# Stick-breaking attention over two key blocks with a flagged full pass, and seven products for all k, q, v and g projections

## The chip, the core and the metric

The kernel runs on one core of a Trainium2 chip. A core has a matrix engine (TensorE, PE in the profile; PEld are its weight loads), a vector engine (VectorE, DVE), a scalar engine for activation functions and copies (ScalarE, ACT), a general engine (GpSimd, POOL) and a sequencer that issues most transfers (SyncE, SP). 16 DMA engines move data between the device's memory and the on-chip buffers. Each engine works through its own instructions in order and waits on semaphores for the others. The metric is the time of one execution on the device in microseconds; lower is better.

## The reference, cut to what matters

The network has two layers over 2048 positions of width 1024. Layer 0 is a gated short convolution. Layer 1 is attention with 8 heads of width 64 which has no softmax: a query's weight on a key is the key's own sigmoid times the product of (1 - sigmoid) over all keys between that key and the query. All keys and values come from one projection, queries and a gate from another, both of layer 0's output.

```python
z = jnp.einsum("bhqd,bhkd->bhqk", qb, kf[:, :, :kl]) * scale
mask = jnp.arange(kl)[None, :] < q_pos[:, None]
log_one_minus = jnp.where(mask, jax.nn.log_sigmoid(-z), 0.0)
rev = lax.cumsum(log_one_minus, axis=3, reverse=True)
weights = jnp.exp(jnp.where(mask, z + rev, -jnp.inf))
outs.append(jnp.einsum("bhqk,bhkd->bhqd", weights, vf[:, :, :kl]))
...
factors = {'norm_kv': 7.745, 'norm_b': 8.0, 'norm_f': 2.922}
```

The factors enlarge the gains of the norms ahead of k and v, of q and g, and of the last norm. Computed from the reference's inputs, the scores z of the last head and block have a standard deviation of 60.

## The kernel before

Positions are reversed on the host, so that the causal direction runs forwards within a row, and cut into four chunks of 512 (`CH`); the width is cut into 8 blocks of 128 (`KD`). Activations lie with the width on the partitions. Each f32 operand of a product is split into a high and a low part (`split`: a copy to ACT's rounding type, then a difference on DVE), and a product of three matmuls (high-high, high-low, low-high) stands for one f32 product (`mm3`).

**Stages.** The mixer's input projection, the convolution and the mixer's output projection run first, over pairs of chunks (0, 1) and (2, 3). Where a pair is taken together, two blocks of weights and two chunks make a 2 by 2 block product, which `fast_unit` does in seven block products instead of eight, from combined operands (`fast_operands`, names op_b and op_t) and combined weights (`fast_weights`: a11, a12, a22, s1 to s4). Each of the seven is 4 k-blocks times three matmuls of 512 columns, so a unit has 84 matmuls where the plain way has 96.

**k, q, v, g.** For chunks 0 and 1, `pair_operands` builds the operands (tag `kq`) and eight units follow: `pair_kq(i)` for a block of k and one of q, `pair_vg(i)` for v and g. For chunks 2 and 3, `norm_1` normalises a chunk, and `proj_k`, `proj_q`, `proj_v` and `proj_g` do plain products (tiles pk, pq, pv, pg; 24 matmuls for each block and chunk). k, q, v and g of all chunks go to device memory (k_d, q_d, v_d, sg_d).

**Attention** (`attention`, lines 1086 to 1146) runs for each chunk c and head h, and within it over all key chunks kc from c down to 0. For each of the four 128-query blocks it computes scores against 512 keys (z), ACT makes sigmoid(-z) (R), POOL masks the diagonal block, and DVE's scan turns R into running products, starting from the carry (cy) of the key chunk before. PE transposes R block by block (wt), the result is split (wth, wtl) and multiplied with v (av). v is stored as differences of neighbouring rows, so the running products alone weigh it. The tiles q2, kt and vv have two buffers each; every other key chunk's k and v go into wraw buffers.

**Output.** `out_b(c)` gates the heads' result (og), multiplies it with the output weights (tiles pob) and adds the residual; `out_norm(c)` normalises and stores. Chunk 3 has its own `out_b_last` and `finish`, whose last part is the tail of the program.

**Order.** Nothing runs as it is recorded. Every operation goes into a `Recorder` under a part's name (`part("a00", attention, 0, 0, ot)` and the like); `PLAN` gives each part a start and an end key, and `order` picks the operation that could start first by a table of costs, and the one with the lower key among equals. The result is one fixed list for each engine. So a change of parts or keys moves instructions throughout the program. All recorded operations have the one source line 355 in the profile, and are told apart by their tiles.

Of the kernel before, what the change touches and what calls it, by code (L numbers as in the profile page):

```python
# [10 lines left out]
F32 = mybir.dt.float32  # L11
# [8 lines left out]
NH = 8  # L20
# [3 lines left out]
NR, NT, NL, NWB, NRAW, NA, NWTS = 13, 4, 5, 8, 4, 16, 2  # L24
# [7 lines left out]
XNL = (0, 3, 6)  # L32
# [29 lines left out]
}  # L62

# [26 lines left out]
class View:  # L90
# [36 lines left out]
    def extent(self):  # L127
# [6 lines left out]
        for name, args, kw in self.steps:  # L134
            if name == "__getitem__":
                both = [x[args[0]] for x in both]
            elif name == "rearrange":
                both = [x.reshape(x.shape[0], -1) for x in both]
# [225 lines left out]
def kernel(  # L364
# [46 lines left out]
    v_first = const.tile([P, NCH, NH // 2, 4], F32, name="v_first")  # L411

# [257 lines left out]
    HOMES = {"b11": ["R"] * 8, "t1": ["R"] * 5 + ["wth"] * 2 + ["wtl"], "t2": ["act"] * 4, "b22": ["act"] * 4,  # L670
# [4 lines left out]
    def operand(c, nm, k, raw, eng=nc.vector):  # L675

        if k == 0:
            fast_b[c, nm] = []
            other = {"t1": "t4", "t4": "t1"} if c == "kq" else {}
# [117 lines left out]
    def share(key, d, gain):  # L797
        if gain is not None:
            split_d[key[0]], split_d[key[1]] = [d["a11"], d["a12"]], [d["a21"], d["a22"]]

    def fast_weights(c, nm, key, srcs=None, gain=None):
# [7 lines left out]
        kept_w = ("a11", "a12", "a21", "a22") if gain is not None else NAMES  # L809
        d = {n: dram.tile([P, 2, Q, P], F32, name=f"sw_{n}_{nm}") for n in kept_w}  # L810
        share(key, d, gain)
        if gain is None:
            split_d[key] = d

        def put(n, raw):
            w[n] = w_tile(f"{n}_{nm}")
            split(w[n][:, 0], w[n][:, 1], raw)
            if n in d:
                nc.sync.dma_start(out=d[n], in_=w[n].bitcast(F32))

        a = raw_blocks(nm, srcs, gain)
        if gain is not None:
            put("a21", a["a21"])
        combine(a, put)
        return w

    def prepare(nm, key, srcs, gain=None):
# [11 lines left out]
        if gain is not None:  # L839
            put("a21", a["a21"])  # L840
# [510 lines left out]
```

## Time and profile before

| | us |
|---|---|
| median of 3 runs | 1653.89 |
| lowest and highest run | 1652.05, 1655.34 |
| span of the profiled execution, first to last instruction | 1652.7 |
| first product of k, q, v, g (pair kq) | 796.7 |
| first score of attention | 963.7 |
| last product of attention with v | 1618.4 |

No time of its own is given for the profiled execution beside its span. The profile lists, for each group of instructions, the tiles (out<-in), the shape, how many there are, how long the group was busy in all, the mean of one in ns, and behind the second bar how long the engine had been idle before them and what ended that wait. A table by stretches gives, for each stretch, each engine's busy time with its count of instructions, then the granted share of PE's clock, the mean busy share of the 16 DMA engines and the GB/s that they moved. The chain of waits is followed back from the last instruction, at each step to what released it. Matmuls overlap each other, so the mean of one is longer than the distance between two.

### The profile page before, as it was taken

To read this page: it belongs to the slowest core of one execution; us is meant where nothing else is said; L and a number is where in the kernel's file an instruction comes from. 1 tells how busy PE (TensorE), PEld (TensorE's weight loads), DVE (VectorE), ACT (ScalarE), POOL (GpSimd) and SP (SyncE) were. 2 spreads that over 40 slices of the span, in tenths; PEclk is the share of its full clock that TensorE was granted. 3 is DMA by queue.
4 is the path that set the end of the run, shared out by engine and by line. 5 is a ranking of instruction groups with operands and counts; after the bars stand their busy time and mean duration, and the time that the engine had idled before them with its cause. 6 is when DMAs were issued, how large, how long until landed. Compare 5 with 4: busy or idle time off the path is not lost. (4 is left out here: it accounts for less than half of the span.)

```text
span 1652.7 us, 24087 instructions
## 1 busy us (share of the span) xinstructions
PE 1614.5 (98%) x7828; PEld 1337.6 (81%) x7828; DVE 1334.0 (81%) x1968; ACT 786.0 (48%) x1483; POOL 487.9 (30%) x684
## 2 busy tenths in 40 slices
PE   7999999999999999999999999999999999999996
PEld 5878888888888887888788878888888888888875
DVE  6999777796765559495977577988999999989995
ACT  6454444443332224242454345655655675756552
POOL 5331000010000201235512132344533344257533
PEclk9999999999999999999999999999999999999997
DMA  9487888889799999999786799998776776699644
GB/s 281 171 268 276 297 280 274 273 272 371 259 315 386 358 372 325 366 339 339 241 283 237 263 353 337 335 312 262 239 237 215 243 236 207 188 339 320 197 144 134
DMA packets 243822, 460.41 MB, mean 279 GB/s; under 512 B 23024, under 2 KB 96752, under 8 KB 243696
## 3 DMA queue, kind: packets, MB, share of 16 engines
q1 hardware_dynamic: 214336, 400.10, 70.4%
q10 hardware_dynamic: 29200, 58.74, 12.1%
q8 instruction: 62, 1.02, 0.2%
q14 instruction: 64, 0.52, 0.1%
q0 software_dynamic: 160, 0.02, 0.1%
HBM read 287.08 MB, written 171.70 MB: 278 GB/s over the span
## 5 line engine op out<-in xcount | busy, mean ns | idle before, releaser
L355 DVE TENSOR_TENSOR_SCAN R<-R,cy,ones 128x512 f32<-128x512 f32 x192 | 247.6, 1316 | 0.9 <-ACT R L355 0.6
L355 ACT CAST wth<-wt 128x512 fp32r<-128x512 f32 (+2 forms) x320 | 154.7, 527 | 159.7 <-PE wt L355 133.2
L355 DVE TENSOR_TENSOR wtl<-wt,wth 128x512 fp32r<-128x512 f32 (+2 forms) x320 | 180.1, 597 | 27.6 <-ACT wth L355 26.0
L355 PE MATMUL z<-kt,q 128*128 128x512 f32 (+2 forms) x640 | 179.7, 378 | 1.0 <-DMA kt<-k_d 0.6
L355 ACT ACTIVATE R<-z 128x512 f32<-128x512 f32 (+2 forms) x320 | 158.7, 548 | 30.8 <-PE z L355 23.7
L355 PE MATMUL wt<-ident,R 128*128 128x128 f32 x1088 | 163.9, 272 | 1.1 <-DVE R L355 1.1
L355 PEld LDWEIGHTS wt<-ident,R 128*128 128x128 f32 x1088 | 132.5, 140 | 20.8 <-DVE R L355 1.8
L355 POOL COPY halo<-p 128x2 f32<-128x2 f32 x32 | 16.1, 503 | 433.5 <-DVE p L355 433.5
L355 POOL COPY cy<-R 128x1 f32<-128x1 f32 x192 | 93.9, 492 | 142.0 <-DVE R L355 135.3
L355 PEld LDWEIGHTS z<-kt,q 128*128 128x128 f32 x640 | 111.7, 189 | 18.7 <-ACT R L355 2.3
L355 PE MATMUL av<-wtl,vv 128*128 128x512 f32 (+1 forms) x320 | 121.6, 384 | 1.8 <-DVE wtl L355 1.8
L355 PE MATMUL av<-wth,vv 128*128 128x512 f32 (+1 forms) x320 | 119.0, 372 | 2.8 <-ACT wth L355 2.3
L355 POOL TENSOR_TENSOR acc_x<-acc_x,sq_x 128x512 f32<-128x512 f32 x52 | 75.2, 1449 | 122.4 <-ACT sq_x L355 113.9
L355 DVE TENSOR_TENSOR_SCAN R<-R,ones 128x512 f32<-128x512 f32 (+3 forms) x128 | 103.9, 844 | 3.0 <-POOL R L355 2.3
L355 PE MATMUL pob<-og,whl_ob 128*128 128x512 f32 x360 | 103.8, 401 | 0.9 <-DVE x L355 0.9
L355 POOL TENSOR_SCALAR_AFFINE_SELECT R<-R 128x128 f32<-128x128 f32 x128 | 72.7, 585 | 107.4 <-ACT R L355 104.2
L355 PE MATMUL fa_C<-op_t,whl_s_C 128*128 128x512 f32 x336 | 83.4, 389 | 0.0
L355 PE MATMUL fa_B<-op_t,whl_s_B 128*128 128x512 f32 x336 | 82.0, 389 | 0.0
L355 PEld LDWEIGHTS av<-wth,vv 128*128 128x128 f32 x320 | 60.1, 188 | 19.3 <-ACT wth L355 6.6
L355 PEld LDWEIGHTS pob<-og,whl_ob 128*128 128x128 f32 x360 | 65.2, 188 | 12.6 <-DVE x L355 1.4
L355 PEld LDWEIGHTS av<-wtl,vv 128*128 128x128 f32 x320 | 60.2, 188 | 17.2 <-DVE wtl L355 5.2
L355 PEld LDWEIGHTS fa_B<-op_t,whl_s_B 128*128 128x128 f32 x336 | 63.0, 188 | 13.2
(586 smaller groups left out, 3747.0 us busy)
## 6 DMA issues: line engine op xcount, KB each, us to landing
vv<-v_d ACTq DMA_DIRECT2D x80, 256.0 KB, 4.2
kt<-k_d ACTq DMA_DIRECT2D x80, 256.0 KB, 4.8
sw_s_C<-whl_s_C SPq DMA_DIRECT2D x32, 512.0 KB, 3.8
sw_s_B<-whl_s_B SPq DMA_DIRECT2D x32, 512.0 KB, 3.5
whl_s_o<-sw_s_o SPq DMA_DIRECT2D x32, 512.0 KB, 6.2
q<-q_d ACTq DMA_DIRECT2D x64, 256.0 KB, 5.9
sw_a_C<-whl_a_C SPq DMA_DIRECT2D x24, 512.0 KB, 3.6
sw_a_B<-whl_a_B SPq DMA_DIRECT2D x24, 512.0 KB, 3.0
```

What stands on the lines that cost most here:

```text
L355: getattr(o.engine.engine, o.name)(*map(real, o.args), **{k: real(v) for k, v in o.kw.items()})
```

## The change

Three things change, and the plan's keys with them.

**Attention over two blocks.** `attend` takes the place of `attention` in the main program. A block of 128 queries sees only its own block of keys and the next older one: 256 scores for each query, one scan of 256 columns from 1.0, no carry. For a head and chunk that is 8 score matmuls of 256 columns, 2 sigmoids and 2 masks (each over both near blocks of a tile), 4 scans, 8 transposes (7 in chunk 0), 2 splits, and 10 products with v of 256 or 128 columns. In chunks 1 to 3 the block that belongs to the chunk before is loaded in addition. POOL copies the last column of each scan into `left`, except for the query block that has no older keys.

**A flag.** `any_left` takes the maximum of `left`, adds up over the partitions whether it is above zero, and keeps it as an integer. Behind the whole main program every engine reads it; if it is not zero, attention over all keys and the output of all chunks run again.

**Seven products throughout.** Chunks 2 and 3 are done as a second pair in the same way as chunks 0 and 1; the plain projections are gone. All seven pieces of a unit's weights are stored for the second pass, where four plain pieces were stored before.

```diff
-NR, NT, NL, NWB, NRAW, NA, NWTS = 13, 4, 5, 8, 4, 16, 2
+NR, NT, NL, NWB, NRAW, NA, NWTS = 12, 4, 5, 8, 4, 16, 2
...
-    "p23": (980.0, 992.4), "g2": (972.8, 1247.5), "xn3": (991.3, 1236.4), "p30": (1188.9, 1257.1),
+    "kq22": (1033.7, 1056.5), "vg22": (1041.7, 1093.2), "kq23": (1097.9, 1102.9), "vg23": (1152.5, 1157.2),
...
+    left = const.tile([P, NCH * NH * 4], F32, name="left")
+    nc.gpsimd.memset(left, 0.0)
...
-    HOMES = {"b11": ["R"] * 8, "t1": ["R"] * 5 + ["wth"] * 2 + ["wtl"], ...
+    HOMES = {"b11": ["R"] * 8, "t1": ["R"] * 4 + ["wth"] * 2 + ["wtl"] * 2, ...
...
-        kept_w = ("a11", "a12", "a21", "a22") if gain is not None else NAMES
-        d = {n: dram.tile([P, 2, Q, P], F32, name=f"sw_{n}_{nm}") for n in kept_w}
+        split_d[key] = d = {n: dram.tile([P, 2, Q, P], F32, name=f"sw_{n}_{nm}") for n in NAMES}
...
+    def attend(c, h, ot):
...
+        if c:
+            nc.scalar.dma_start(out=kt[:, CH:CH + P].bitcast(F32), in_=k_d[c - 1][h][:, 0:P])
+            nc.scalar.dma_start(out=vt[:, 4].bitcast(F32), in_=v_d[c - 1][hb][:, hi_, 0, :, :])
+        else:
+            nc.gpsimd.memset(kt[:, CH:CH + P].bitcast(F32), 0.0)
+        rs = []
+        for i in range(2):
+            ps = psum.tile([P, CH], F32, name=f"z_{nm}_{i}", tag="z", bufs=NZ)
+            for j in range(2):
+                qi = 2 * i + j
+                for m in range(2):
+                    nc.tensor.matmul(ps[:, 2 * j * P:2 * (j + 1) * P], q2[:, m, qi * P:(qi + 1) * P], kt[:, qi * P:(qi + 2) * P],
+                                     start=m == 0, stop=m == 1, skip_group_check=True)
...
+            nc.scalar.activation(r, ps, AF.Sigmoid, scale=-0.125)
+            near = r.rearrange("p (j k) -> p j k", j=2)[:, :, 0:P]
+            nc.gpsimd.affine_select(out=near, in_=near, pattern=[[0, 2], [1, P]], base=0, channel_multiplier=-1,
+                                    compare_op=ALU.is_gt, fill=1.0)
+            for j in range(2):
+                own = r[:, 2 * j * P:2 * (j + 1) * P]
+                nc.vector.tensor_tensor_scan(out=own, data0=own, data1=ones[:, 0:1].to_broadcast([P, 2 * P]), initial=1.0,
+                                             op0=ALU.mult, op1=ALU.mult)
+            n = 1 if c == 0 and i else 2
+            at = 4 * (c * NH + h) + 2 * i
+            nc.gpsimd.tensor_copy(left[:, at:at + n], r[:, 2 * P - 1:2 * P * n:2 * P])
...
+        for i, places in enumerate((((1, 0), (1, 1), (2, 1), (2, 2)), ((3, 2), (3, 3), (0, 0), (4, 3)))):
+            if c == 0 and i:
+                places = places[:3]
...
+    def any_left():
+        most = const.tile([P, 1], F32, name="most")
+        nc.vector.reduce_max(out=most, in_=left, axis=mybir.AxisListType.X)
...
+        nc.tensor.matmul(ps[:, 0:1], ones, some, start=True, stop=True)
+        nc.vector.tensor_copy(flag, ps[:, 0:1])
...
-    part("xk", pair_operands)
+    for c in (0, 2):
+        part(f"xk{c}", pair_operands, c)
         for i in range(4):
-            part(f"p{c}{i}", proj, c, i)
-        part(f"g{c}", proj_gate, c)
+            part(f"kq{c}{i}", pair_kq, c, i)
+            part(f"vg{c}{i}", pair_vg, c, i)
...
-                part(f"a{c}{h}", attention, c, h, ot)
+                part(f"a{c}{h}", attend, c, h, ot)
...
+    some = tc.nc.values_load(flag.real()[0:1, 0:1])
+    with tc.If(some != 0, preferred_fallthrough_block=False):
...
+                    attention(c, h, ot)
...
+            out_b(c)
+            out_norm(c)
```

Three places in the order of the program. On PE, in the stage where k, q, v and g of chunks 2 and 3 are made, before: pv and pg are plain products of chunks 2 and 3 with normalised operands xn, and z, wt and av belong to attention heads.

```order
L355 MATMUL pv_2_9535<-xn_5_8907,whl_v_2_1_9249 128x512
L355 MATMUL z_1_0_0_9696<-kt_1_0_9420,q_1_1_9296 128x512 x2
L355 MATMUL z_1_0_1_9702<-kt_1_0_9420,q_1_1_9296 128x512
L355 MATMUL av_2_9706<-wth_2_0_3_9694,vv_2_0_9520 128x512
L355 MATMUL pv_2_9535<-xn_5_8907,whl_v_2_1_9249 128x512
L355 MATMUL wt_2_0_1_9715<-ident,R_2_0_0_9593 128x128
L355 MATMUL wt_2_0_1_9715<-ident,R_2_0_1_9608 128x128
L355 MATMUL z_1_0_1_9702<-kt_1_0_9420,q_1_1_9296 128x512
L355 MATMUL pg_1_9681<-xn_0_8717,whl_gg_1_0_9276 128x512
```

On PE after, at the border between the two pairs: fa_vg_0 and fd_vg_0 are units of pair (0, 1) near its end, fd_kq_2 is the first of pair (2, 3), and op_t_('kq', 2) the new operands.

```order
L353 MATMUL fa_vg_0_8746<-op_t_('kq', 0)_2_7630,whl_a_vg_0_8677 128x512
L353 MATMUL fa_vg_0_8746<-op_t_('kq', 0)_3_7663,whl_a_vg_0_8677 128x512
L353 MATMUL fa_vg_0_8746<-op_t_('kq', 0)_3_7675,whl_a_vg_0_8677 128x512
L353 MATMUL fa_vg_0_8746<-op_t_('kq', 0)_3_7663,whl_a_vg_0_8677 128x512
L353 MATMUL fd_kq_2_8901<-op_t_('kq', 2)_0_8807,whl_s_kq_2_8797 128x512 x3
L353 MATMUL fd_kq_2_8901<-op_t_('kq', 2)_1_8812,whl_s_kq_2_8797 128x512 x3
L353 MATMUL fd_kq_2_8901<-op_t_('kq', 2)_2_8833,whl_s_kq_2_8797 128x512
L353 MATMUL fd_kq_2_8901<-op_t_('kq', 2)_2_8845,whl_s_kq_2_8797 128x512
L353 MATMUL fd_kq_2_8901<-op_t_('kq', 2)_2_8833,whl_s_kq_2_8797 128x512
L353 MATMUL fd_vg_0_8722<-op_b_('kq', 0)_0_7283,whl_s_vg_0_8916 128x512 x3
```

The products of chunks 2 and 3 stand in units directly behind those of chunks 0 and 1, with no attention between them; the first scores of attention come some 400 matmul rows later, in the last unit of the second pair.

On ACT, in the attention stage, before: q, kt and vv are the loads of a head, R the sigmoids, wth the first half of a split.

```order
L355 ACTIVATE R_4_1_1_13747<-z_4_1_1_13698 128x512
L355 ACTIVATE R_4_1_2_13753<-z_4_1_2_13710 128x512
L355 ACTIVATE R_4_1_3_13757<-z_4_1_3_13735 128x512
L355 DMA vv_7_0_13764<-v_d_3_212 128x512
L355 COPY ot_3_13468<-av_7_13497 64x512
L355 CAST wth_6_0_3_13777<-wt_6_0_3_13762 128x512
L355 CAST wth_6_0_2_13783<-wt_6_0_2_13769 128x384
L355 ACTIVATE R_4_0_0_13788<-z_4_0_0_13774 128x512
L355 ACTIVATE R_4_0_1_13794<-z_4_0_1_13781 128x512
L355 ACTIVATE R_4_0_2_13802<-z_4_0_2_13786 128x512
L355 ACTIVATE sq_x_13811<-x1o_3_10277 128x512
L355 DMA q_3_1_13818<-q_d_0_205 64x1024
```

On ACT after, in the attention of chunk 0.

```order
L353 CAST wth_4_0_10436<-wt_4_0_10416 128x512
L353 ACTIVATE R_6_0_10444<-z_6_0_10428 128x512
L353 CAST wth_4_1_10455<-wt_4_1_10419 128x384
L353 ACTIVATE R_6_1_10462<-z_6_1_10439 128x512
L353 DMA q_0_7_10471<-q_d_3_198 64x1024 x2
L353 DMA kt_7_10453<-k_d_7_170 128x512
L353 COPY ot_2_10363<-av_4_10450 64x512
L353 CAST wth_0_0_10498<-wt_0_0_10486 128x512
L353 DMA vv_6_10501<-v_d_3_214 128x512
L353 CAST wth_0_1_10508<-wt_0_1_10493 128x384
```

A load now stands on ACT after every second or third copy, where before there were four to eight computing instructions between two.

On SP, at the end of the program, before and after: x_3 are the result tiles of chunk 3.

```order
L355 DMA out_dram<-x_3_1_15756 128x512
L355 DMA out_dram<-x_3_5_16223 128x512
L355 DMA out_dram<-x_3_6_16273 128x512
L355 DMA out_dram<-x_3_4_16092 128x512
L355 DMA out_dram<-x_3_7_16443 128x512
L1346 UNCONDITIONAL_BRANCH
```

```order
L353 DMA out_dram<-x_3_5_13065 128x512
L353 DMA out_dram<-x_3_6_13102 128x512
L353 DMA out_dram<-x_3_4_13059 128x512
L353 DMA out_dram<-x_3_7_13153 128x512
L1338 TENSOR_LOAD flag
L1339 COMPARE_AND_BRANCH
L1339 UNCONDITIONAL_BRANCH
```

Behind the last store, SP now reads the flag, compares and branches; the same three instructions stand at the end of every engine's list, ahead of the block that runs if the flag is set.

More of the change, by code (lines that the diff above doesn't have):

```diff
@@ L30 @@
 NLIN, NZ, NWT, NAV = 2, 3, 2, 1
-XNL = (0, 3, 6)
 YLP = (2, 5)
@@ L137, in extent @@
             elif name == "rearrange":
-                both = [x.reshape(x.shape[0], -1) for x in both]
+                if args[0] == "p (j k) -> p j k":
+                    both = [x.reshape(x.shape[0], kw["j"], -1) for x in both]
+                else:
+                    both = [x.reshape(x.shape[0], -1) for x in both]
             elif name == "unsqueeze":
@@ L678, in operand @@
             fast_b[c, nm] = []
-            other = {"t1": "t4", "t4": "t1"} if c == "kq" else {}
+            other = {"t1": "t4", "t4": "t1"} if isinstance(c, tuple) and c[0] == "kq" else {}
             home[nm] = list(HOMES[other.get(nm, nm)])
@@ L817, in put @@
             split(w[n][:, 0], w[n][:, 1], raw)
[L818 to L824, printed above, removed]
+            nc.sync.dma_start(out=d[n], in_=w[n].bitcast(F32))
+        combine(raw_blocks(nm, srcs, gain), put)
         return w
     def prepare(nm, key, srcs, gain=None):
-        split_d[key] = d = {n: dram.tile([P, 2, Q, P], F32, name=f"sw_{n}_{nm}") for n in NAMES + ("a21",)[:gain is not None]}
-        share(key, d, gain)
+        split_d[key] = d = {n: dram.tile([P, 2, Q, P], F32, name=f"sw_{n}_{nm}") for n in NAMES}
         def put(n, raw):
@@ L836, in put @@
                 nc.sync.dma_start(out=d[n][:, m], in_=hl[m].bitcast(F32))
-        a = raw_blocks(nm, srcs, gain)
-        if gain is not None:
-            put("a21", a["a21"])
-        combine(a, put)
+        combine(raw_blocks(nm, srcs, gain), put)
     def prepare_out(u):
@@ L1146, in attention @@
                 nc.vector.tensor_add(ot[osl, :], ot[osl, :], av[osl, :])
+    flag = const.tile([P, 1], I32, name="flag")
+    def any_left():
+        most = const.tile([P, 1], F32, name="most")
+        nc.vector.reduce_max(out=most, in_=left, axis=mybir.AxisListType.X)
+        some = const.tile([P, 1], F32, name="some")
+        nc.vector.tensor_scalar(out=some, in0=most.bitcast(I32), scalar1=0, scalar2=None, op0=ALU.is_gt)
+        ps = st("p_left")
+        nc.tensor.matmul(ps[:, 0:1], ones, some, start=True, stop=True)
+        nc.vector.tensor_copy(flag, ps[:, 0:1])
     og_t = {}
@@ L1313 @@
                 nc.sync.dma_start(out=og_d[c][hb], in_=ot)
+    part("fl", any_left)
     for c in range(3):
@@ L1323 @@
         nc.emit(ops)
+    some = tc.nc.values_load(flag.real()[0:1, 0:1])
+    with tc.If(some != 0, preferred_fallthrough_block=False):
+        og_t.clear()
+        acc_b.clear()
+        for c in range(NCH):
+            for hb in range(NH // 2):
+                ot = sb.tile([P, CH], F32, name=f"all_ot_{c}_{hb}", tag="ot", bufs=2)
+                for h in (2 * hb, 2 * hb + 1):
+                    attention(c, h, ot)
+                nc.sync.dma_start(out=og_d[c][hb], in_=ot)
+            out_b(c)
+            out_norm(c)
 _INS = ["xT", "norm_a", "w_in_a", "conv_a", "w_out_a", "norm_kv", "w_kv", "norm_b", "w_in_b", "w_out_b", "norm_f"]
```

123 lines of the change are left out of this document (55 added, 68 removed), and 47 rows, old and new, of the table PLAN.

## The prediction

> **What bounds the kernel now.** I read the page's first part, then the busy time by stretch, then the DMA queues.
>
> ```profile
> span 1652.7 us, 24087 instructions
> PE 1614.5 (98%) x7828; PEld 1337.6 (81%) x7828; DVE 1334.0 (81%) x1968; ACT 786.0 (48%) x1483; POOL 487.9 (30%) x684
> ```
>
> PE is busy for 98% of the span, so PE work that goes shortens the kernel until something else is full. The stretches say what is next. They are cut where the program changes: output projection of the mixer (645 to 805), k, q, v, g of chunks 0 and 1 (to 964), then attention together with k, q, v, g of chunks 2 and 3 and the last projection, and the tail from 1618.
>
> ```profile
> core 0: us, PE busy (x) PEld busy (x) DVE busy (x) ACT busy (x) POOL busy (x), PEclk, DMA share, GB/s
> 645.00:805.00 160.00, 157.61 (x702) 128.93 (x701) 113.64 (x181) 54.33 (x95) 57.14 (x41) 1.00 0.91 327
> 805.00:964.00 159.00, 158.68 (x723) 130.23 (x722) 114.68 (x183) 72.49 (x127) 38.89 (x46) 1.00 0.79 272
> 964.00:1110.00 146.00, 142.66 (x768) 119.28 (x767) 125.97 (x178) 81.21 (x175) 52.09 (x95) 1.00 1.01 332
> 1110.00:1286.00 176.00, 175.17 (x959) 147.29 (x958) 160.00 (x215) 99.16 (x210) 67.43 (x134) 1.00 0.78 242
> 1286.00:1618.00 332.00, 328.97 (x1817) 276.22 (x1815) 316.57 (x428) 206.53 (x414) 163.06 (x243) 1.00 0.72 233
> 1618.00:1652.70 34.70, 19.06 (x86) 15.46 (x84) 20.22 (x37) 8.66 (x14) 11.45 (x9) 0.76 0.36 121
> ```
>
> Two things stand there. Until 1618 PE is the bound in every stretch. And the 16 DMA engines are already full in one of them: from 964 to 1110 their share is 1.01 at 332 GB/s. Before 805 the change alters little (the same matmuls in a somewhat different order), so I leave that part as it is, to within 5 us.
>
> **The change part by part.** How far apart two matmuls start is read from the chain of waits, which runs through PE there.
>
> ```profile
> 1171.70 1.62 PE pq L355 x7
> 1177.23 0.87 PE wt L355 x8
> L355 PE MATMUL z<-kt,q 128*128 128x512 f32 x448 | 142.2, 409 | 0.9 <-DMA kt<-k_d 0.6 <-ACT R L355 0.2
> L355 PE MATMUL z<-kt,q 128*128 128x384 f32 x64 | 17.2, 341 | 0.0
> L355 PE MATMUL z<-kt,q 128*128 128x256 f32 x128 | 27.4, 291 | 0.1
> L355 PE MATMUL wt<-ident,R 128*128 128x128 f32 x1088 | 163.9, 272 | 1.1 <-DVE R L355 1.1
> L355 PE MATMUL pk<-xn,whl_k 128*128 128x512 f32 x192 | 57.7, 404 | 0.0
> ```
>
> A product of 512 columns takes 1.62/7 = 0.231 us of PE, a transpose 0.87/8 = 0.109. (The mean in a group's row, 409 ns, overlaps its neighbours.) Estimated in proportion, 384 columns are 0.174 and 256 are 0.116.
>
> Attention on PE, before: the scores are 448 x 0.231 + 64 x 0.174 + 128 x 0.116 = 129 us, the products with v have the same 640 shapes, another 129, and 1088 transposes x 0.109 are 119; together 377. After: 256 score products of 256 columns are 30 us, 248 transposes 27, 192 products with v of 256 columns 22, and 112 of 128 columns. No row has this last kind. Its nearest rows are the transpose of 128 columns, 0.109, and the 512-column product, 0.231; I take 0.109, 12 us, and keep 26 as the other end. Together 91, so **286 us of PE go**. The carries between chunks go too, with their 192 copies on POOL. One R buffer fewer costs nothing that I can see: a head takes 2 of the 12, where a chunk of a head took 4 of 13.
>
> The projections of chunks 2 and 3 are 4 groups of 192 products now and 8 units of 84 afterwards: 768 - 672 = 96, x 0.231 = **22 us of PE**. They gain operands to be built (16 differences and 28 splits, 44 on DVE, about 30 us at 0.68 each, beside PE, which has 155 us of products there) and lose 8 splits of weights (the a21 pieces). The same hand-over from one operand set to the next stands in the trace around 805 (mixer output to k and q), and PE is busy for 158.68 of 159 us there, so I charge 2 us, 20 at most, which is one unit of 84 products if the operands come a unit late.
>
> By PE alone the kernel would end at 1652.7 - 286 - 22 = 1345. That is the low end, since other engines must now do their part in less time. Sixteen units, 8 as today and 8 new, take twice the 159 us from 805, and attention begins when they end, at **1123**, because scores, carries and operands share the buffers R, wth, wtl, q2, kt and vv. What stands after 1123, engine by engine:
>
> ```profile
> L355 ACT ACTIVATE R<-z 128x512 f32<-128x512 f32 x224 | 127.6, 612 | 27.9 <-PE z L355 21.9 <-PE wt L355 4.5 <-POOL cy L355 0.4
> L355 ACT CAST wth<-wt 128x512 fp32r<-128x512 f32 x224 | 123.5, 591 | 118.1 <-PE wt L355 101.7 <-DVE R L355 6.9 <-DMA q<-q_d 3.5
> L355 ACT COPY ot<-av 64x512 f32<-64x512 f32 x32 | 18.6, 581 | 25.6 <-PE av L355 22.6 <-DMA whl_gg<-sw_a_vg 2.6
> L355 ACTq DMA_DIRECT2D q<-q_d x64: 451/463/1126, 945.8 to 1542.3; - x64
> L355 ACTq DMA_DIRECT2D kt<-k_d x80: 321/327/1559, 936.7 to 1564.4; - x80
> L355 DVE TENSOR_TENSOR_SCAN R<-R,ones 128x256 f32<-128x256 f32 x32 | 21.9, 685 | 0.2
> L355 DVE TENSOR_TENSOR wtl<-wt,wth 128x512 fp32r<-128x512 f32 x224 | 144.9, 677 | 20.9 <-ACT wth L355 19.6
> L355 DVE TENSOR_TENSOR ot<-ot,av 64x512 f32<-64x512 f32 x32 | 21.7, 678 | 7.3 <-ACT ot L355 6.9
> L355 POOL TENSOR_SCALAR_AFFINE_SELECT R<-R 128x128 f32<-128x128 f32 x128 | 72.7, 585 | 107.4 <-ACT R L355 104.2 <-PE z L355 2.6
> L355 POOL TENSOR_TENSOR acc_x<-acc_x,sq_x 128x512 f32<-128x512 f32 x52 | 75.2, 1449 | 122.4 <-ACT sq_x L355 113.9 <-DVE x L355 8.2
> L355 POOL COPY cy<-R 128x1 f32<-128x1 f32 x192 | 93.9, 492 | 142.0 <-DVE R L355 135.3 <-DVE t_x L355 2.7
> ```
>
> PE: attention 91, 384 products of the output projection x 0.231 = 89, small ones 5: 185 us. DVE: 128 scans x 0.685 = 88, 64 splits x 0.677 = 43, 32 sums x 0.678 = 22, and some 60 sums and splits of the output at 0.68 = 41: 194. ACT: 64 x 0.612 + 64 x 0.591 + 32 x 0.581 = 96, its 64 issues of q x 0.463 and 112 of k and v x 0.327 = 66, and some 75 copies, squares and scalings of the output, at 0.6 like the rows above, 45: 207. POOL: 64 masks of twice the size, between 0.585 and 1.17 each, 37 to 75; 64 small copies of what is left x 0.492 = 31; 83 two-operand operations of the output x 1.449 = 120: 188 to 226. All of them stand near 200, and none above 226.
>
> The transfers are more. A head of chunks 1 to 3 loads q (0.52 MB), k and v (0.26 each) and two blocks of 0.07: 1.18 MB; a head of chunk 0 1.05. That is 36.7 MB. The SP queue moves another 59 MB after the last weight of the units (weights of the output projection 4.2 MB a chunk, residual, x2 out and back, result 2.1 each, gates and heads). **96 MB**.
>
> ```profile
> 720.00:740.00 20.00, 20.00 (x98) 16.87 (x97) 19.63 (x50) 7.68 (x14) 3.55 (x3) 1.00 1.03 399
> q1 hardware_dynamic: 214336, 400.10, 70.4%
> q10 hardware_dynamic: 29200, 58.74, 12.1%
> ```
>
> Over the whole program, the sizes of all transfers added up, SP's queue (q1) goes from 400.1 to 404.2 MB and ACT's (q10) from 58.7 to 36.7: 4% less in a fifth less time.
>
> At what rate? 332 GB/s at a full share from 964 to 1110, where both queues run as they will; 327 at 0.91, so 359 at a full one, from 645 to 805; 399 for 20 us. I take 340, nearest to the first. 96 MB / 340 GB/s = 282 us. The Trainium skill's page "DMA: Bandwidth & Descriptors", section Specifications, gives about 358 GB/s as the limit of the memory for a core. By that figure the stage would take 268 us and the sum below would be 14 us less; the 399 of one row is above it, so here it is no cap.
>
> The sum: the stage's transfers begin a unit (20 us) ahead of 1123, at 1103. 1103 + 282 = 1385. In the tail the engines idle: today's last 34.7 us move at a share of 0.36, which loses 22 us; more results are still going out there afterwards, so I charge half, 11: 1396. At the end every engine reads the flag and branches. No row has this; between nothing and the 5.9 us that a load takes to land (its row is below) I take 2: the flag was written long before, nothing but the branch is queued behind the instruction that reads it, and only SP, last to finish, reads it on the path: **1398**. The page gives the profiled execution no time of its own beside its span; the median is 1.2 us above the span, less than the rounding here. The other added operations (one maximum, one product, a copy of 128 x 1) are off the path.
>
> The units before 1123 bear the same check: they move 106 MB (nine of it because all seven pieces of a unit's weights are now stored for the second pass) in 318 us, 333 GB/s, which is just what the full stretch carried. This is cover without reserve: every GB/s that is missing there is paid at once, 3 us for one per cent.
>
> **The rivals.** *PE stays the bound.* If DMA carries 399 as from 720 to 740, the stage is 241 us and the end 1103 + 241 + 11 + 2 = 1357, next to the 1345 of PE. For it: short peaks. Against it: the share of 1.01 at 332.
>
> *The chain of a head decides.* q, k and v have two buffers each, where now far blocks borrow four more from wraw. One head runs load, scores, ACT, mask, scan, transposes, splits, products, sum.
>
> ```profile
> q<-q_d ACTq DMA_DIRECT2D x64, 256.0 KB, 5.9
> ```
>
> 5.9 to land + 0.5 + 1.2 + 1.8 + 2.7 + 0.9 + 1.2 + 1.4 + 1.0 + 1.3 = 18 us, less about 2 where two tiles overlap; with two heads in flight 8 us a head, 32 heads 256, then the tail of 35 and the first head's 16: 1123 + 256 + 51 + 2 = 1432. A load that waits for its buffer also holds up the sigmoids and copies queued behind it on ACT, and PE waits for those. Against it: loads are issued ahead of the scores of the head before.
>
> *A cold PE.* In the last stretch PE is busy for 19.06 of 34.7 us and its granted clock is 0.76. If attention has such gaps, its 185 us stretch; at 0.76 to 245, which decides nothing, and only under 185/282 = 0.66 does PE set the end; at half the clock it is 370 and the end 1123 + 370 + 2 = 1495. The Trainium skill's "TensorE: Matmul & The Clock Gate", Part 1, says that an idle window of some 3.4 us halves the clock; the trace's last row agrees in kind.
>
> *The flag is set.*
>
> ```profile
> L355 DVE TENSOR_TENSOR_SCAN R<-R,cy,ones 128x512 f32<-128x512 f32 x192 | 247.6, 1316 | 0.9 <-ACT R L355 0.6
> ```
>
> Then all of attention and three chunks of output run again behind the branch. The price is at least what DVE now spends on three rows of attention, 248 us of scans, 145 of splits and 22 of sums, 415 in all, so 1813 or more: slower than before. It decides as soon as one of the products over a query's last 128 to 255 keys is above zero. From the reference's inputs the largest of them has the logarithm -1803, since the scores spread by 60; f32 ends at -103. So the flag should be zero, unless the chip's sigmoid does not fall as the function does, which no row shows.
>
> **How the numbers follow.** Forecast 0.50; PE bound 0.22; chain of a head 0.21; cold PE 0.04; flag set 0.03. The likeliest time is 1398. The range takes the PE sum of 1345 and the chain with a late operand set, 1432 + 20, so 1345 to 1452, and leaves out the last two cases and a little of the others. Differences under 0.2% are no change to this measurement. Faster 0.965, same 0.005, slower 0.03.
>
> **What would show it.** The DMA share over the attention stage: near 1.0 at 330 to 360 GB/s bears me out. PE busy over 95% there: the first rival. Both under 0.85, with ACT or PE waiting for q, k or v: the second. A clock under 0.7 on the page: the third. Instructions of `attention` in the trace: the flag. The units should end near 1123; if that is off by over 10 us, or the stage's 96 MB do not take about 280 us, that step was wrong.

## The result

The changed kernel takes **1444.0 us** (median of four runs, 1440.5 to 1445.0) against 1653.0 for the kernel before: the ratio is **0.873, 95% interval 0.871 to 0.875**. The prediction was 1398, from 1345 to 1452. The sign and the stage that bounds were right, and the mechanism was right in the main; the time lies inside the range, but 46 us above the forecast; most of what follows looks for these 46 us. The profiled execution has a span of 1443.1 us, so that positions in its trace can be set against the terms of the prediction directly.

The first lines of the page and its two busiest DMA queues, after:

```profile
span 1443.1 us, 19169 instructions
PE 1342.1 (93%) x6174; PEld 1105.6 (77%) x6174; DVE 978.1 (68%) x1557; ACT 579.2 (40%) x999; POOL 379.2 (26%) x447
q1 hardware_dynamic: 216352, 404.30, 80.9%
q10 hardware_dynamic: 22288, 36.72, 9.5%
```

PE lost 272 us of busy time and is busy for 93% of the span, no longer 98%. The queues moved 404.3 and 36.7 MB, where 404.2 and 36.7 had been counted beforehand. The same kind of table by stretch as before, cut where the stages of the changed kernel change:

```profile
core 0: us, PE busy (x) PEld busy (x) DVE busy (x) ACT busy (x) POOL busy (x), PEclk, DMA share, GB/s
645.00:805.00 160.00, 158.56 (x709) 130.22 (x707) 101.57 (x170) 53.70 (x92) 53.07 (x40) 1.00 0.94 337
805.00:964.00 159.00, 154.40 (x697) 126.25 (x698) 122.15 (x191) 74.62 (x132) 53.22 (x48) 1.00 0.97 340
964.00:1123.00 159.00, 157.57 (x717) 128.89 (x716) 66.76 (x102) 50.12 (x87) 14.91 (x33) 1.00 0.95 329
1123.00:1402.00 279.00, 219.48 (x1188) 182.84 (x1187) 186.96 (x309) 130.81 (x228) 135.93 (x193) 0.87 0.98 294
1402.00:1443.10 41.10, 18.68 (x82) 15.54 (x80) 18.04 (x37) 7.93 (x13) 21.38 (x17) 0.70 0.63 211
```

Up to 1123 PE is the bound as forecast (157.57 of 159 us) and the transfers just keep up. From 1123 to 1402, attention and the output projection, the DMA engines take over: share 0.98, while PE, DVE, ACT and POOL are busy for 219, 187, 131 and 136 of 279 us. That is the forecast picture but for one number: the engines carry 294 GB/s here (300 at a full share), not 340. PE's clock fell to 0.87, so that its 219 us would be 191 at full clock (204 with the last row), against 185 forecast for all that stands behind 1123.

What PE waited for in that stage, by the view of the waits:

```profile
engine line waited for: us in total, times, longest us
PE z L353 <- DMA kt<-k_d: 16.5, 9, 2.7
PE av L353 <- ACT wth L353: 9.3, 7, 4.3
PE wt L353 <- DVE R L353: 9.0, 10, 2.8
```

The largest entry is a load of k, as it must be if transfers set the pace; but the waits for steps within a head (ACT's split, DVE's scan) are together longer. So two theories were open, and the first experiments set them against each other. **A**: the stage's bytes bound it, at 294 GB/s. **B**: the chain of a head, with two buffers each for q, k and v, bounds it.

### The profile page after: what moved, and what is told of

It reads as the page before. It is cut to its first block, busy times and chain, and to the rows that moved or that the text cites. A ratio compares the mean times of both kernels' runs of the same rounds, so it can differ in the third digit from the quotient of the medians.

```text
span 1443.1 us, 19169 instructions
## 1 busy us (share of the span) xinstructions
PE 1342.1 (93%) x6174; PEld 1105.6 (77%) x6174; DVE 978.1 (68%) x1557; ACT 579.2 (40%) x999; POOL 379.2 (26%) x447
## 4 chain that ended last, share of the span: by engine, by line
PE 72%; DMA 11%; DVE 7%; issue 3%; ACT 2%; POOL 2%; SPq 0%; ACTq 0%; POOLq 0%; DVEq 0%
PE fa_B L353 11%; PE fa_C L353 10%; PE fa_kq L353 6%; PE fa_o L353 6%; PE fd_B L353 5%; PE fd_C L353 5%; PE fa_vg L353 5%; PE fd_kq L353 3%; PE fd_o L353 3%; PE fd_vg L353 3%; PE fe_C L353 3%; PE fe_B L353 3%; DMA kt<-k_d 2%; PE pob L353 2%; DMA q<-q_d 2%
## 5 line engine op out<-in xcount | busy, mean ns | idle before, releaser
L353 DVE TENSOR_TENSOR_SCAN R<-R,ones 128x256 f32<-128x256 f32 x128 | 89.5, 739 | 23.1 <-POOL R L353 23.0
L353 PE MATMUL z<-kt,q 128*128 128x256 f32 x256 | 54.6, 343 | 24.2 <-DMA kt<-k_d 16.5
L353 PEld LDWEIGHTS fa_C<-op_t,whl_s_C 128*128 128x128 f32 x336 | 63.0, 188 | 13.2
L353 PEld LDWEIGHTS z<-kt,q 128*128 128x128 f32 x256 | 44.7, 233 | 29.0 <-issue 24.0
L353 PE MATMUL wt<-ident,R 128*128 128x128 f32 x248 | 54.4, 319 | 10.7 <-DVE R L353 9.0
L353 DVE TENSOR_TENSOR wtl<-wt,wth 128x512 fp32r<-128x512 f32 x64 | 41.8, 668 | 25.0 <-ACT wth L353 24.6
L353 DVE SCALAR_TENSOR_TENSOR cv<-p,cw,cv 128x512 f32<-128x512 f32 x64 | 50.1, 783 | 6.9 <-ACT cv L353 5.2
L353 PE MATMUL av<-wth,vv 128*128 128x256 f32 (+1 forms) x152 | 41.3, 304 | 14.0 <-ACT wth L353 9.3
L353 PEld LDWEIGHTS wt<-ident,R 128*128 128x128 f32 x248 | 34.1, 159 | 21.2 <-DVE R L353 14.7
L353 PE MATMUL fa_B<-op_b,whl_a_B 128*128 128x512 f32 x168 | 42.7, 400 | 2.7 <-DVE cv L353 2.7
```

What stands on the lines that cost most here:

```text
L353: getattr(o.engine.engine, o.name)(*map(real, o.args), **{k: real(v) for k, v in o.kw.items()})
```

## Experiments

Every time below is a median; the ratio to the kernel before, with its 95% interval, stands behind it. The changed kernel's is 0.873, 0.871 to 0.875. The planner lays out each variant anew, so a small edit also moves instructions elsewhere: in the traces, some 750 to 1400 of PE's 6174 instructions stand in another place than in the changed kernel for the runs on x2, buffers, q once, one queue, q in one transfer of 128 partitions, and both byte edits. Only three variants keep its order exactly: q in two transfers of 64 partitions with other rows, without the flag, and the short program behind the branch. What a new order alone is worth was not measured for the others, so differences of a few us there say little.

**Fewer bytes: x2 stays in SBUF.**

```diff
-            x = sb.tile([P, CH], F32, name=f"x1o_{c}_{ob}", tag="og", bufs=KD)
+            x = x2_t[c][ob // 2][:, ob % 2, :].bitcast(F32)
...
-            nc.sync.dma_start(out=x2_d[c][ob], in_=x)
...
-            t = ld512(f"x2r_{c}_{k}")
-            nc.sync.dma_start(out=t, in_=x2_d[c][k])
+            t = x2_t[c][k // 2][:, k % 2, :].bitcast(F32)
```

> Changed kernel, but x2 of chunks 0 to 2 stays in SBUF until its norm is known, in place of being stored and loaded again: 12.6 MB fewer of the 96.7 MB that move after 1103. Theory A, the transfers bound the attention stage and move 292 GB/s: 12.6 MB are 43 us, so about 1400 us, share still near 1.0, rate still near 292. Theory B, the chain of a head (load, scores, mask, scan, transposes, products) with two buffers for q, k and v decides: no load of a head changes, so 1444 within 5 us.

Measured: 1444.8 us (0.874, 0.872 to 0.877). Nothing was gained. Theory A, as put, falls. The stage in two parts, of the changed kernel first and of this one second:

```profile
1123.00:1340.00 217.00, 162.27 (x882) 135.31 (x880) 142.69 (x225) 100.27 (x176) 94.15 (x147) 0.85 0.97 288
1340.00:1400.00 60.00, 55.21 (x295) 45.76 (x295) 43.85 (x83) 29.95 (x51) 39.79 (x45) 0.94 0.99 317
```

```profile
1123.00:1340.00 217.00, 165.55 (x895) 138.56 (x894) 150.69 (x231) 103.58 (x183) 106.67 (x158) 0.83 0.98 285
1340.00:1400.00 60.00, 54.66 (x293) 46.49 (x292) 42.82 (x79) 26.36 (x46) 33.07 (x39) 0.89 0.64 194
```

The bytes left the last 60 us, where the share fell from 0.99 to 0.64; up to 1340 the DMA engines were as full as before and PE had done hardly more (166 us for 162). In the last 60 us PE is busy for 55 either way: there it is the bound, with the output's products. Theory **C** follows: the stage has two parts, the first paced by the heads' loads, the second by PE, and only bytes that leave the first part count.

**More buffers for q, k and v.** The tiles kt and vv change as q2 does.

```diff
-        q2 = sb.tile([P, 2, CH], F32R, name=f"q2_{nm}", tag="q2", bufs=2)
+        q2 = sb.tile([P, 2, CH], F32R, name=f"q2_{nm}", tag="act", bufs=NA)
...
```

> Changed kernel, but the tiles of q, k and v in attention take their buffers from the 16 of the operands (free by then), in place of two each. Theory A: same bytes at the same rate, 1444 within 6 us, share near 1.0. Theory B: loads land ahead of their head, PE's waits for k and q (20 us in the stage) go, and 20 to 40 us less, 1404 to 1424.

Measured: 1446.7 (0.875, 0.873 to 0.877). Theory B, in the form of too few buffers, falls: PE's wait for k is as long as before.

```profile
PE z L353 <- DMA kt<-k_d: 15.7, 12, 4.7
```

**q loaded once.**

```diff
-        for i in range(2):
-            nc.scalar.dma_start(out=q2[i * 64:(i + 1) * 64, :, :].bitcast(F32), in_=q_d[c][hb][hi_ * 64:(hi_ + 1) * 64, :, :])
+        nc.scalar.dma_start(out=q2[0:64, :, :].bitcast(F32), in_=q_d[c][hb][hi_ * 64:(hi_ + 1) * 64, :, :])
+        nc.scalar.copy(q2[64:128, :, :], q2[0:64, :, :].bitcast(F32))
```

> Changed kernel, but q of a head is loaded once, to 64 partitions, and copied to the other 64 by ScalarE, in place of being loaded twice: 8.4 MB fewer, one ACT copy of 64x1024 more and one ACT issue fewer for each of 32 heads. Theory A at 292 GB/s: 29 us less, about 1415. Theory B: the copy, about 1 us, lies in the chain of every head; with two heads in flight 0 to 16 us more, 1444 to 1460. Beside it: if the 256 ns of q's 4096-byte packets on ACT's queue (197 on SP's) come from the same source being read twice at once, their mean falls to about 200 here; if they come from the 64 partitions or from the queue, it stays near 256.

Measured: 1427.7 (0.864, 0.861 to 0.867), 16 us less, with 8.4 MB less where the first edit's 12.6 MB gave nothing. Neither forecast was met (1415, or 1444 and more), but it fits C: q's bytes lie in the first part. The packets of q kept their length, as the table below shows, so reading one source twice is not what makes them slow.

**One queue.** All loads of `attend` change in this way.

```diff
-        nc.scalar.dma_start(out=kt[:, 0:CH].bitcast(F32), in_=k_d[c][h])
+        nc.sync.dma_start(out=kt[:, 0:CH].bitcast(F32), in_=k_d[c][h])
...
```

> Changed kernel, but the loads of q, k and v in attention are issued on SP's queue with all other transfers, not on ACT's. Same bytes, same pieces. If two queues in turn slow the packets (theory A1): 4096 bytes from 256 to about 197 ns, 2048 from 111 to 98, together about 22 us, so 1422 and a rate near 312. If the rate belongs to the pieces themselves (theory A2): packet times stay, 1444 within 5 us. If ACT, held up by loads that wait for buffers, sets the pace (theory B2): the packet times stay, the share of DMA rises, PE's waits for ACT fall, and 10 us or more go.

Measured: 1438.3 (0.870, 0.868 to 0.872): 6 us less, and the intervals just touch. On the one queue the 4096-byte packets of q and of weights together took 228 ns on the mean; with 197 for the weights' that is about 252 for q's. So it is not the queue that makes q's packets slow either. Two other signs of theory B2 did come: from 1123 to 1400 the share rose to 1.01 at 305 GB/s, and PE's wait for ACT's split fell from 9.3 to 1.4 us. ACT held up by its loads may be worth these 6 us, not the 10 or more of the forecast.

**The shape of q's load.** Two kernels load the same rows to the same partitions, once in one transfer of 128 partitions, once in two of 64.

```diff
...
-        for i in range(2):
-            nc.scalar.dma_start(out=q2[i * 64:(i + 1) * 64, :, :].bitcast(F32), in_=q_d[c][hb][hi_ * 64:(hi_ + 1) * 64, :, :])
+        nc.scalar.dma_start(out=q2.bitcast(F32), in_=q_d[c][hb])
```

The part cut there keeps the planner's keys of attention as if both transfers were still there; the order comes out otherwise all the same.

> Changed kernel, but q's tile is loaded by one transfer of 128 partitions (both heads of the pair of rows) in place of two of 64 partitions: same bytes, same 4096-byte packets, one ACT issue fewer a head. It leaves out the doubling of q, so that heads multiply with rows of their neighbour too. If the 256 ns of those packets come from the 64 partitions: about 197 ns here, 15 us less of all 16 DMA engines in the first part, 1429 to 1436. If they come from something else in q's loads: still near 256, 1444 within 5 us.

```diff
-            nc.scalar.dma_start(out=q2[i * 64:(i + 1) * 64, :, :].bitcast(F32), in_=q_d[c][hb][hi_ * 64:(hi_ + 1) * 64, :, :])
+            nc.scalar.dma_start(out=q2[i * 64:(i + 1) * 64, :, :].bitcast(F32), in_=q_d[c][hb][i * 64:(i + 1) * 64, :, :])
```

> Control for the run with one transfer of 128 partitions: the same rows of both heads go to the same partitions, but in two transfers of 64 partitions each, as in the changed kernel; the order of the instructions is the changed kernel's own. Like that run it leaves out the doubling of q. If the 64 partitions of a transfer make its packets slow: 250 to 260 ns for q's 4096 bytes, 1444 within 5 us. If reading one source twice made them slow, or the order that came out a little otherwise: near 190 ns and 1418 to 1430.

Measured: one transfer of 128 partitions 1421.3 (0.859, 0.856 to 0.863), two of 64 partitions 1446.4 (0.874, 0.872 to 0.877). The stage and ACT's queue in it (packets, MB, share of 16 engines), with two of 64 first and one of 128 second:

```profile
1123.00:1400.00 277.00, 221.91 (x1190) 185.59 (x1190) 187.59 (x311) 131.46 (x229) 133.12 (x195) 0.86 0.99 296
q10 hardware_dynamic: 20320, 34.49, 47.1%
```

```profile
1123.00:1400.00 277.00, 225.87 (x1242) 187.33 (x1240) 205.91 (x328) 138.04 (x240) 151.04 (x204) 0.89 0.91 313
q10 hardware_dynamic: 19601, 33.85, 36.2%
```

The same queue moves nearly the same bytes in 36.2% instead of 47.1% of the engines' time, 82 instead of 103 ns a packet (share x 16 x 277 us over the packets). Split by size, from the packet records of the traces between 1123 and 1400:

```
mean ns of a packet                ACT 4096 (q)   ACT 2048   SP 2048   SP 4096
changed kernel                         256          111        98        197
two of 64, other rows                  267          111        98        195
q once, 64 partitions                  265          110        93        194
one of 128 partitions                  191           93        92        186
```

With transfers of 128 partitions q's packets are as fast as SP's, and the packets of k and v, whose own shape did not change, get faster with them. One transfer of 64 partitions a head (q once) has slow packets as well, so it is not the pair of transfers. So it is the 64 partitions of a transfer that cost, and they cost others too. Weighed with the counts of the run with two of 64, the shorter packets save (267 - 191) x 3810 + (111 - 93) x 7680 + (98 - 92) x 15360 + (195 - 186) x 2963 ns; over 16 engines that is 34 us on each (an estimate). The run gained 25 us, more than half of the missing 46; the packets suffice for that, but the order differs between the two runs too, and its part of the 25 was not separated. The Trainium skill's page "SBUF — State Buffer", in "Door 1: The DMA port swizzle" and in "Can I just issue two DMAs to hit both halves?", states just this: partitions 0 to 63 reach 8 of 16 ports, and two transfers to the two halves don't make up for one to all. It gives 196 against 328 GB/s for 1 MiB; the 191 against 267 ns here, beside other transfers, agree in direction with a smaller factor (0.72 against 0.60).

**Both byte edits together** (x2 stays, q once).

> The two edits together: x2 stays in SBUF, and q is loaded once and copied: 21 MB fewer. Alone the first gave nothing and the second about 16 us. Theory C, the stage has two parts with different bounds, the loads of the heads first and PE with the output's products last, and only bytes that leave the first part count: the two add up, 1428 within 5 us. Theory A, rescued (the bytes do bound the stage, and the first edit gave nothing only because q's loads stood in the way): 1400 to 1412, share still above 0.9 to 1380.

Measured: 1432.4 (0.865, 0.861 to 0.868), no better than q once alone.

```profile
1123.00:1340.00 217.00, 180.04 (x957) 151.86 (x956) 158.77 (x248) 136.68 (x219) 110.47 (x164) 0.82 0.82 256
1340.00:1400.00 60.00, 54.40 (x265) 45.20 (x263) 38.05 (x72) 24.11 (x39) 41.81 (x39) 0.91 0.55 181
```

Now the DMA engines are idle for a fifth of the first part and half of the second, no engine is full in the first (PE 180 of 217, at a clock of 0.82), and the stage is hardly shorter. Behind the transfers a second bound stands at once: PE with a lowered clock and waits in it. By the view of the waits, from 1123 to 1402, none that it lists is for a load any more; the longest are for steps within a head, one of them the copy of q (1.0 us a head on ACT) that this variant adds:

```profile
PE wt L353 <- DVE R L353: 18.1, 21, 2.8
PE z L353 <- ACT q L353: 6.7, 6, 1.9
```

PE and DMA both under 0.85 was the prediction's sign for the chain of a head, and here it shows. A, rescued, is out; C's sum is what came.

**The planner's rate.**

```diff
-DMA_RATE, DMA_BEFORE, DMA_AFTER, FLY = 0.36, 1.0, 2.8, 8
+DMA_RATE, DMA_BEFORE, DMA_AFTER, FLY = 0.30, 1.0, 2.8, 8
```

> Changed kernel, one number in the planner: it lays out the order with transfers of 300 GB/s, in place of 360 (the chip gave 292 to 294 in the stage). Theory D, the order is the loss, since it counts on loads that come later than planned: 10 to 20 us less, 1424 to 1434. Theory C: the same work on the same bounds, 1444 within 6 us.

Measured: 1556.8 (0.940, 0.938 to 0.943), 113 us more, which neither theory expected. Most of it arose ahead of attention, whose first score starts at 1201.3 in place of 1114.6:

```profile
645.00:805.00 160.00, 135.79 (x563) 107.19 (x562) 97.50 (x171) 52.70 (x90) 27.62 (x21) 0.94 0.89 306
964.00:1123.00 159.00, 135.04 (x573) 107.62 (x574) 90.06 (x132) 59.29 (x105) 36.50 (x38) 0.92 0.85 300
```

In the changed kernel PE is busy for 159 and 158 us there. The one number lays out the whole program anew, under keys that belong to the old one. So the run says nothing about theory D in attention; it says that an order is worth over 100 us here, and that a variant made under old keys may be held back by its order.

**One part of the change alone: two blocks, plain products.** The kernel before with `attend` in place of `attention`, new plan keys for what follows 964, no flag:

```diff
-                part(f"a{c}{h}", attention, c, h, ot)
+                part(f"a{c}{h}", attend, c, h, ot)
```

> The kernel before with attention over two blocks alone: k, q, v, g of chunks 2 and 3 keep their plain products, and attention runs beside them as before; the flag is left out, the order is a new plan. By PE: 1652.7 - 286 = 1367 or more. By the transfers: from 964 on the kernel before moved 173 MB, 22 of them fewer here, 151 MB; at 292 to 332 GB/s 455 to 517 us and half a tail, 1430 to 1490. If the projections hide the heads' loads better than the changed kernel does (theory C: two parts, of which one starves PE), the time is at the low end of that, and the second part of the change is worth nothing; if PE's 96 products fewer pay, 1465 or more.

Measured: 1451.5 (0.878, 0.876 to 0.881). Its stages:

```profile
964.00:1123.00 159.00, 137.84 (x695) 113.03 (x696) 85.63 (x133) 55.04 (x103) 31.97 (x68) 0.95 1.00 319
1123.00:1340.00 217.00, 201.48 (x1054) 167.06 (x1053) 119.76 (x185) 86.09 (x149) 88.53 (x117) 0.98 1.01 341
```

Here the projections of chunks 2 and 3 run beside attention, and PE and DMA are both nearly full from 1123 to 1340. It is the transfers' forecast, in the lower half of it.

**Without the flag**, and **with a short program behind the branch**.

```diff
-    some = tc.nc.values_load(flag.real()[0:1, 0:1])
-    with tc.If(some != 0, preferred_fallthrough_block=False):
...
```

> Changed kernel without the read of the flag and the branch with full attention behind it (it leaves out what would be done if weight were left, which these inputs don't need). The prediction charged 2 us. If so: 1440 to 1443, and from the landing of the last result to the end of the span as in the kernel before. If the read and the branch lie behind the last transfer and cost more: down to 1438. If instruction loading for the branch disturbs the rest: more than 6 us.

```diff
-        for c in range(NCH):
-            for hb in range(NH // 2):
...
-            out_b(c)
-            out_norm(c)
+        ot = sb.tile([P, CH], F32, name="all_ot_0_0", tag="ot", bufs=2)
+        for h in range(2):
+            attention(0, h, ot)
+        nc.sync.dma_start(out=og_d[0][0], in_=ot)
```

> Changed kernel with the flag read and the branch, but behind the branch stands attention for two heads of chunk 0 only (it leaves out the rest of what would be done if weight were left, which these inputs don't need). Without flag and branch the kernel took 1435 against 1444; of these 9 us its trace and the changed kernel's show some 3 after the last result. If the read and the jump themselves cost the 9 us: 1444 within 3. If the length of the program behind the branch does (instructions that are loaded, other places in memory): 1435 to 1439.

Measured: 1435.0 (1429 to 1440; 0.868, 0.866 to 0.870) without, 1439.0 (1436 to 1446; 0.870, 0.868 to 0.873) with a short one. The medians don't decide between the forecasts for the short program, as its interval touches both. The ends of the traces say more. SP's eight last stores in the kernel before, the changed one, the one without flag and the one with the short branch (start, time from the first issue to the end of the last):

```profile
1643.78 4.81 SPq L355 DMA_DIRECT2D out_dram<-x  x8
```

```profile
1429.06 7.18 SPq L353 DMA_DIRECT2D out_dram<-x  x8
```

```profile
1418.83 4.81 SPq L353 DMA_DIRECT2D out_dram<-x  x8
```

```profile
1426.56 7.17 SPq L353 DMA_DIRECT2D out_dram<-x  x8
```

From the first issue to the end of the span it is 8.9 us in the kernel before (1652.7 - 1643.8), 14.1 in the changed one, 8.7 without flag (span 1427.6) and 10.8 with the short branch (span 1437.4). So the flag costs 5.1 us at the end: 2 for reading and jumping (on SP 2.8 us behind its stores, or 2.7 with the short branch, where they stand among the stores), and 3 more with the long program behind the branch. In the records of the changed kernel three of the eight issues take 1.1 to 1.8 us each; without flag and with the short branch none takes over 0.41. The same holds in every trace of this case: with the long program (ten kernels) the end takes 13.4 to 15.4 us, the longest of the eight issues 0.84 to 2.04 us and PE's own jump 4.1 to 4.2 us; with the short one it is 10.8, 0.41 and 0.18, and in the three kernels without a branch the end takes 8.6 to 8.9 us and no issue over 0.41. That the 3 us come from the length is argued and not shown: there is one short program, and with it SP's read also stands in another place. The two profiled executions, with and without flag, are 15.5 us apart, 10 of them within the stage (the last product with v ended at 1391, not 1401, in the same order of instructions); with runs of the kernel without flag 11 us apart, and the fastest of them profiled, that may be scatter, and it stays open.

**A version that beats both.** Two blocks beside the plain products as above, with the flag, and both byte edits:

> A version that may beat the changed kernel: attention over two blocks with the flag, but plain products for k, q, v, g of chunks 2 and 3, beside which attention runs (as in the run with two blocks alone, 1451, whose DMA share was 1.01 at 338 GB/s from 1123 to 1400 with the PE clock at 1.0), and the two edits that took 21 MB away. If the transfers bound that order, 21 MB / 338 GB/s = 62 us less, cut off by PE at about 1362 us busy and the tail's 25 us: 1390 to 1400. If its order is bound by PE's gaps as in the changed kernel (where 12.6 of these MB gave nothing): 1430 to 1451.

Measured: **1414.1** (0.855, 0.854 to 0.857), 30 us less than the changed kernel, between the two forecasts. (The PE clock of two blocks alone, put at 1.0 there, was 0.94 over 1123 to 1400.)

```profile
964.00:1340.00 376.00, 354.79 (x1864) 294.81 (x1863) 212.91 (x337) 181.97 (x299) 138.26 (x201) 0.97 0.99 330
1340.00:1385.00 45.00, 39.96 (x194) 31.26 (x192) 32.30 (x62) 18.02 (x31) 28.98 (x30) 0.92 0.43 139
1385.00:1412.30 27.30, 7.30 (x33) 6.76 (x32) 9.29 (x22) 4.65 (x8) 6.26 (x6) 0.57 0.23 81
```

DMA and PE are nearly full together up to 1340 (0.99, and 355 of 376 us), at a PE clock of 0.97; what is left is the dependent end. The byte edits, worth 12 to 16 us where attention runs alone, take some 40 off here (from 1451.5 without flag to 1414.1 with it).

## Why the prediction was right, and what it missed

**Up to 1123: right.** The first product of k and q starts at 792.8 (796.7 before), the first score at 1114.6, against 1123 forecast; the units' last product ends at 1136.8, over the 10 us that the prediction allowed, as the first heads were started among its units; only 5 us of the units' products lie behind 1123. From 805 to 1123 PE was busy for 312 of 318 us. The transfers were the cover that they were said to be, 329 to 340 GB/s against 333.

**PE's loss: right.** 272 us of busy time went. The stage's 219 us at a clock of 0.87 hold 28 us that only the clock adds; without them 300 went, against 308 forecast. That the 22 us of the seven products would be earned in full is not what the runs show: two blocks alone against the changed kernel without flag, 1451.5 against 1435.0, leaves 16 for them, under an order for the former that was laid out once and not improved.

**The engines' sums: right to about a tenth for PE, DVE and ACT** (from 1123 to the end 204 at full clock against 185, 205 against 194, and for ACT without its issues 139 against 141), **high for POOL** (157 against 188 to 226). All three of POOL's terms were smaller: the two-operand operations 104 against 120, the small copies 22 against 31, and the mask of 256 elements just under the low end of its bounds, 37:

```profile
L353 POOL TENSOR_SCALAR_AFFINE_SELECT R<-R 128x256 f32<-128x256 f32 x64 | 35.2, 554 | 63.9 <-ACT R L353 63.5
```

**The transfers' rate: the term that was mis-sized.** "332 GB/s at a full share from 964 to 1110 ... I take 340." The bytes were right: 299 us at 294 GB/s (1103 to 1402) and 41.1 at 211 make 96.6 MB, 96 forecast (its "a fifth less time" was 15% by its own forecast, which changes nothing). At a share of 0.98 the engines carried 294, 300 at a full one; by the prediction's own sign, about 280 us for the 96 MB, that step was wrong. With 294 in place of 340 the prediction's own sum gives 1103 + 96/0.294 + 11 + 2 = 1443, which is what was measured. Why 294: by the packet records, q's loads were none of the bytes from 645 to 805 of the kernel before (359 at a full share), 5 of 48 MB from 964 to 1110 (332), and 15 of 82 MB in the changed kernel from 1123 to 1400 (301 at a full share). In two blocks alone they were 9 of 93 MB over the same time, at 338. The more of them, the lower the rate. With q in transfers of 128 partitions a full share is worth 313/0.91 = 344.

**But the rate alone is not the cause of all 46 us**, although the sum closes with it; that it closes is partly luck. By the same sum 12.6 MB fewer would have given 1400, and 1444.8 was measured. Nor does the range hold the time by the forecast's own sum: its upper end of 1452 came from a rival, the chain of a head (1432 + 20). Once the rate is mended the time is 1421, not 1398: the share falls to 0.91, and 0.09 x 277 = 25 us of DMA time stay empty. The prediction let the transfers be full from 1103 to the end. What takes their place is a milder form of two rivals together: PE at a clock of 0.85 and 0.94 in the stage's two parts, and heads whose steps wait for one another, with more buffers of no use. The runs show that this second bound is there (21 MB fewer gave no more than 8.4); how it divides between clock and chain was not separated.

**The end: 5 us of flag for 2 forecast.** The 2 were right for the read and the jump; what came with the long program behind it was left out. **The rivals**: *PE stays the bound* fell with the stage's 219 of 279 us; *the flag is set* did not come about, as no instruction of `attention` is in the trace.

## What to carry to other kernels

Before a rate is taken from a full stretch, see which transfers fill it: here loads that cover only 64 partitions slowed themselves and their neighbours, and the stretch to be forecast may hold more of them. When a stage turns from one engine to another, removing what is full in it is worth only as much as the next bound leaves, so look for what is second (here PE's gaps) before summing bytes. Work with spare PE time and work with spare DMA time belong beside each other: in the fastest version attention beside the projections kept PE busy for 355 of 376 us with the DMA engines at 0.99, where attention behind them left PE at 219 of 279 beside a share of 0.98.

## What was not expected of the hardware

Transfers to 64 partitions make packets of other transfers slower: k's and v's 2048 bytes took 111 ns beside them and 93 without. It is not in proportion: with half as many of them (q once) it was still 110, and 96 in two blocks alone, where they are a tenth of the bytes. And a block of program that is skipped seems to cost by its length: 14.1 us from the first of the last stores to the end with the long one, 10.8 with a short one, 8.7 with none.
